# Asking once for the sums of an up pair at a group border

## The chip, the cores and the metric

The kernel runs on one core of a Trainium2 chip. TensorE (PE) multiplies, VectorE (DVE), ScalarE (ACT) and GpSimd (POOL) do the rest, and SyncE (SP) and POOL issue most transfers. The metric is the device time of one execution in microseconds; the time before is the median of three executions.

## The reference

An encoder trunk of four layers over 512 tokens of 1024 features, in float32. Each layer has a token mixer (a convolution module, a neighbourhood attention, a retention, and a convolution module again) and then a channel mixer, the same in all four:

```python
def conv_ffn(h, w_up, dw_w, dw_b, w_down):
    u = dwconv(h @ w_up, dw_w, dw_b)          # 1024 -> 2 x 2816, three taps along the tokens
    val, gate = jnp.split(u, 2, axis=-1)
    return (jax.nn.gelu(gate) * val) @ w_down # 2816 -> 1024
```

with a root-mean-square norm ahead of it and the result added to x. The change is in this channel mixer alone.

## The kernel before, in words

The kernel keeps x on the chip with features on partitions: eight tiles of 128 x 512. Float32 products are made of three matmuls on a high and a low part: ACT casts an operand to its high part (L167, L191), DVE subtracts to get the low part (L168, L192), and PE runs high x high, high x low and low x high (L181 to L183). Some of the up matrices get their low part from a transfer that adds into it on its way (L177, on POOL's queue), and PE uses that part last (L316).

The channel mixer, `ffn`, has 44 blocks of 128 hidden features, taken in 22 pairs j (value and gate). `ups_of(j)` makes pair j; `mids` then runs the three taps and the gate over finished pairs. Two parts of the down product, `down(q, ...)`, are run in between, after pair 8 (9 in the second layer) and after pair 16; these places are called borders here, first and second. Down products, and the four up pairs of each layer that the table `UPS` names, are made with seven products of half blocks instead of eight. For that the weights are needed in sums. `sums` asks for them: a load into `ws` (512 KB, L471, on SP), a transfer that adds another 512 KB into it (L474, on POOL's queue, which waits for that load), and a load of 256 KB into `wq` (L475, on SP). `weights` makes the rest: it loads the plain weights into `wr` (L158), splits them (L167, L168), adds on DVE (L484, and L488 into `wq`) and splits the sums (L191, L192). There are three buffers for `ws` and one for `wq`.

`fetch_sums(j)` calls `sums` one pair ahead and puts what it gets into the dictionary `ahead`, from which `up_macro(j)` takes it. `ups_of(j)` starts with `fetch_sums(j + 1)`.

At a border `down` ends with two calls: `late()`, which runs the taps of pair j, and `filler()`, which is `ups_of(j + 1)`. Then its last output is finished (`finish`: two products, L538 and L515 on DVE, and an addition to x in memory, L539 and L516, on POOL's queue). After that the loop over j goes on and calls `ups_of(j + 1)` once more. Its products were made already, so it makes none; but its first line asks for the sums of pair j + 2 again, and where pair j + 2 is in `UPS` that replaces what the first call had got. That is so for the first pair of `UPS` behind each border: pairs 10 (11 in the second layer) and 18, so twice in each layer.

The order of the work on each engine is set at compile time by a scheduler with a simulated timeline; each engine then works its list in order and waits on semaphores. `issue_after` in `sums` keeps its transfers behind a given load.

Of the kernel before, what the change touches and what calls it, by code (L numbers as in the profile page):

```python
# [77 lines left out]
UPS = ((10, 12, 18, 19), (11, 13, 18, 19), (10, 12, 18, 19), (10, 12, 18, 19))  # L78
# [5 lines left out]
def tile_trunk(  # L84
# [213 lines left out]
    def ffn(l, after):  # L298
        with ExitStack() as st:
# [3 lines left out]
            def up(n):  # L303
                c = n // 2 + FT * (n % 2)
                ps = bank(psa)
                acc = n in ACC
                wh, wl = load_w_acc(f_up[l, c], D) if acc else load_w(f_up[l, c], D)
                for k in range(KD):
                    s = slice(k * P, (k + 1) * P)
                    if acc:  # L310
                        nc.tensor.matmul(ps, wh[:, s], xhi[k], start=k == 0, stop=False)  # L311
                        nc.tensor.matmul(ps, wh[:, s], xlo[k], start=False, stop=False)  # L312
                    else:
                        mm3(ps, wh[:, s], wl[:, s], xhi[k], xlo[k], k == 0, k == KD - 1)
                for k in range(KD if acc else 0):
                    nc.tensor.matmul(ps, wl[:, k * P:(k + 1) * P], xhi[k], start=False, stop=k == KD - 1)  # L316
                if n == 3 and l == 1:
                    stats1(state["spare"])
                if n == S2[l]:
                    stats2()  # L320
                    scale_first()
                if n == SCALED[l] - 1:
                    scale_rest()
                return ps
# [12 lines left out]
            def combos(p):  # L337
                e, o = x[2 * p], x[2 * p + 1]
                c = hp.tile([P, D], F32, tag="ws", name=nm("cx"), bufs=NWS)
                q = [c[:, i * 256:(i + 1) * 256] for i in range(4)]  # L340
                nc.vector.tensor_tensor(q[0], e[:, 256:], e[:, :256], SUB)
                nc.vector.tensor_tensor(q[1], o[:, :256], e[:, :256], SUB)
                nc.vector.scalar_tensor_tensor(q[2], o[:, :256], -1.0, q[0], MUL, SUB)
                nc.vector.scalar_tensor_tensor(q[3], q[2], -1.0, o[:, 256:], MUL, SUB)
                cl[p] = hp.tile([P, D], F32R, tag=f"cl{p}", name=nm("cl"))
                for k, h in ((2 * p, slice(0, T)), (2 * p + 1, slice(T, D))):
                    ch[k] = const.tile([P, T], F32R, tag=f"x{k}", name=nm("ch"))
                    split(c[:, h], ch[k], cl[p][:, h])
# [9 lines left out]
            open_macro, ahead = [], {}  # L358
# [7 lines left out]
            def finish_up():  # L366
                if open_macro:
                    w, v, s12 = open_macro.pop()
                    uprod(v[:, :256], w["sg"], 2, False)
                    uprod(v[:, 256:], w["a12"], 3, True)  # L370
                    nc.vector.tensor_tensor(s12, v, s12, ADD)

            def up_macro(j):
                w = weights(*ahead.pop(j))
                xb, v = bank(psa), bank(psa)
                xc = xb[:, :256]
                s12, u2 = t512(), t512()
                uprod(xc, w["a11"], 1, True)
                nc.scalar.copy(s12[:, 256:], xc)
                uprod(v[:, 256:], w["a22"], 6, True)  # L380
                uprod(xc, w["s2"], 0, False)
                nc.scalar.copy(s12[:, :256], xc)
                uprod(v[:, :256], w["s1"], 4, True)
                uprod(xc, w["s3"], 5, False)
                finish_up()
                nc.scalar.activation(u2.rearrange("p (h t) -> p h t", h=2),
                                     xc.unsqueeze(1).broadcast_to([P, 2, 256]), AF.Copy, scale=-1.0)
                nc.vector.tensor_tensor(u2, u2, v, SUB)
                open_macro.append((w, v, s12))
                return [s12, u2]  # L390
# [75 lines left out]
            def sums(src, gate=None):  # L466
                n = src.shape[-1] // 4
                r13 = hp.tile([P, D], F32, tag="ws", name=nm("ws"), bufs=NWS)
                sg = hp.tile([P, D], F32, tag="wq", name=nm("wq"))
                with tc.issue_after(gate.ins) if gate else ExitStack():  # L470
                    nc.sync.dma_start(  # L471
                        r13[:, :2 * n].rearrange("p (b n) -> p b n", b=2),
                        src[:, 2 * n:3 * n].unsqueeze(1).broadcast_to([P, 2, n]))
                    nc.gpsimd.dma_start(r13[:, :2 * n], src[:, :2 * n], accum_op=ADD)  # L474
                    nc.sync.dma_start(sg[:, n:2 * n], src[:, 3 * n:])  # L475
                return src, r13, sg
# [109 lines left out]
            done, n = 0, 2  # L586
# [6 lines left out]
                    done += 1  # L593

            def fetch_sums(j):
                if j in UPS[l]:
                    ahead[j] = sums(f_us[l, UPS[l].index(j)], state["load"])

            def ups_of(j):
                nonlocal n  # L600
                fetch_sums(j + 1)
                if j in UPS[l]:
                    ups.extend(up_macro(j))
                    n += 2
                while n < 2 * j + 2:
                    ups.append(up(n))
                    finish_up()
                    n += 1
                if j in COMBO:
                    combos(COMBO.index(j))  # L610

            starts = {2 * p1 + (l == 1 and q == 0): q for q, (_, p1) in enumerate(PARTS)}
            for j in range(1, FT):
                ups_of(j)
                w0 = down_w(0, starts[j], state["load"]) if j in starts else None
                if n > S2[l]:
                    mids(j)
                if w0:
                    down(starts[j], w0, lambda: mids(j + 1), lambda: ups_of(j + 1))
# [685 lines left out]
    kind, l = seq[0]  # L1305
# [177 lines left out]
```

## Time and profile before

| | us |
|---|---|
| three executions | 2617.16, 2610.37, 2615.33 |
| median | 2615.33 |
| the profiled execution: its time | 2619.64 |
| its span, first to last instruction | 2617.6 |
| granted TensorE clock, mean over it | 0.988 |

Views of the profile used below: the page (busy time of each engine, DMA queues, the chain of work that ended last), the waits (engine, line, what it waited for; us in total, how often, longest), the chain in order of time (start us, us, what), the timeline of one engine (start us, us, engine, line, operation, tiles; in brackets the idle time before it and what ended it), and the windows (a stretch; its length; busy us of PE, PEld, DVE, ACT and POOL, with the number of instructions; the granted clock; the DMA share; GB/s). "SPq" and "POOL ... DMA" are instructions that issue a transfer; how long it takes to land is in other rows. A line such as L168 is that of a helper and stands for many places.

### The profile page before, as it was taken

To read this page: it belongs to the slowest core of one execution; us is meant where nothing else is said; L and a number is where in the kernel's file an instruction comes from. 1 tells how busy PE (TensorE), PEld (TensorE's weight loads), DVE (VectorE), ACT (ScalarE), POOL (GpSimd) and SP (SyncE) were. 2 spreads that over 40 slices of the span, in tenths; PEclk is the share of its full clock that TensorE was granted. 3 is DMA by queue.
4 is the path that set the end of the run, shared out by engine and by line. 5 is a ranking of instruction groups with operands and counts; after the bars stand their busy time and mean duration, and the time that the engine had idled before them with its cause. 6 is when DMAs were issued, how large, how long until landed. Compare 5 with 4: busy or idle time off the path is not lost.

```text
span 2617.6 us, 38827 instructions
## 1 busy us (share of the span) xinstructions
PE 2543.1 (97%) x15166; PEld 2192.1 (84%) x15166; DVE 1824.9 (70%) x3004; ACT 1264.4 (48%) x1763; POOL 393.9 (15%) x484
## 2 busy tenths in 40 slices
PE   9999999999999999999999999999989999999989
PEld 7888888889998888888888888789888888789787
DVE  7976867577877785657656566685747887686755
ACT  5455545464556554445332423464535445554543
POOL 1214110103421111110000000211011121101010
PEclk9999999999999999999999999999999999999999
DMA  7736776643333567674222222577665672477674
GB/s 240 234 93 189 189 169 173 157 146 97 96 90 109 144 170 172 157 183 123 81 81 72 81 74 75 133 185 183 167 149 140 204 228 83 132 189 173 163 162 138
DMA packets 128521, 381.18 MB, mean 146 GB/s; under 512 B 15521, under 2 KB 18465, under 8 KB 128337
## 3 DMA queue, kind: packets, MB, share of 16 engines
q1 hardware_dynamic: 94144, 283.59, 34.8%
q0 software_dynamic: 32896, 92.39, 19.0%
q10 hardware_dynamic: 1296, 2.72, 0.3%
q8 instruction: 119, 1.95, 0.3%
q14 instruction: 66, 0.53, 0.1%
HBM read 344.07 MB, written 30.79 MB: 143 GB/s over the span
## 4 chain that ended last, share of the span: by engine, by line
PE 80%; DMA 8%; DVE 7%; ACT 3%; issue 2%; POOL 0%; DVEq 0%; SPq 0%; ACTq 0%; POOLq 0%
PE ps L182 19%; PE ps L183 19%; PE ps L181 19%; PE ps L316 3%; PE ps L312 3%; PE ps L311 3%; PE ps L187 3%; PE ps L186 3%; PE ps L188 3%; DMA wr<-in_f_down 2%; DMA wq<-in_f_us 2%; DVE wl L168 2%; DMA wq<-in_f_down 2%; DMA wl<-in_f_up 1%; PE ps L743 1%
## 5 line engine op out<-in xcount | busy, mean ns | idle before, releaser
L167 ACT CAST wh<-wr 128x1024 fp32r<-128x1024 f32 (+1 forms) x310 | 318.0, 1028 | 546.4 <-PE ps L182 264.4
L183 PE MATMUL ps<-xh,wl 128*128 128x512 f32 (+1 forms) x1248 | 486.4, 391 | 11.6 <-DVE wl L168 11.6
L168 DVE TENSOR_TENSOR wl<-wr,wh 128x1024 fp32r<-128x1024 f32 (+1 forms) x307 | 370.6, 1207 | 177.4 <-ACT wh L167 165.9
L182 PE MATMUL ps<-xl,wh 128*128 128x512 f32 (+1 forms) x1248 | 488.2, 391 | 0.3 <-DVE xl L253 0.3
L181 PE MATMUL ps<-xh,wh 128*128 128x512 f32 (+1 forms) x1248 | 486.1, 390 | 0.8 <-ACT wh L167 0.8
L183 PEld LDWEIGHTS ps<-xh,wl 128*128 128x128 f32 x1248 | 235.2, 189 | 67.1 <-DVE wl L168 15.2
L181 PEld LDWEIGHTS ps<-xh,wh 128*128 128x128 f32 x1248 | 235.2, 189 | 54.7 <-ACT wh L167 1.7
L182 PEld LDWEIGHTS ps<-xl,wh 128*128 128x128 f32 x1248 | 235.4, 189 | 52.5 <-DVE xl L253 1.1
L183 PE MATMUL ps<-Hh,wl 128*128 128x256 f32 (+1 forms) x734 | 224.8, 314 | 9.2 <-DVE wl L168 8.8
L182 PE MATMUL ps<-Hl,wh 128*128 128x256 f32 (+1 forms) x734 | 226.8, 313 | 5.6 <-DVE Hl L192 5.6
L181 PE MATMUL ps<-Hh,wh 128*128 128x256 f32 (+1 forms) x734 | 222.5, 315 | 4.9 <-ACT wh L167 2.8
L311 PE MATMUL ps<-xh,wh 128*128 128x512 f32 x416 | 164.7, 396 | 1.3 <-ACT wh L175 1.3
L312 PE MATMUL ps<-xl,wh 128*128 128x512 f32 x416 | 164.4, 395 | 0.0
L187 PE MATMUL ps<-wl,xh 128*128 128x256 f32 (+1 forms) x512 | 159.8, 313 | 1.8 <-DVE wl L168 1.8
L186 PE MATMUL ps<-wh,xh 128*128 128x256 f32 (+1 forms) x512 | 159.8, 315 | 1.1 <-ACT xh L250 1.1
L188 PE MATMUL ps<-wh,xl 128*128 128x256 f32 (+1 forms) x512 | 159.8, 313 | 0.0
L183 PEld LDWEIGHTS ps<-Hh,wl 128*128 128x128 f32 x734 | 141.3, 195 | 18.8 <-DVE wl L168 11.7
L181 PEld LDWEIGHTS ps<-Hh,wh 128*128 128x128 f32 x734 | 140.8, 195 | 17.0 <-ACT wh L167 6.9
L182 PEld LDWEIGHTS ps<-Hl,wh 128*128 128x128 f32 x734 | 141.6, 193 | 14.6 <-DVE Hl L192 7.2
L488 DVE TENSOR_TENSOR wq<-ws,wq 128x512 f32<-128x512 f32 x48 | 33.1, 689 | 138.8 <-DMA wq<-in_f_down 94.3
L181 PE MATMUL ps<-Hh,h 128*128 128x256 f32 x384 | 111.7, 291 | 15.7 <-DVE t L538 15.2
L316 PE MATMUL ps<-xh,wl 128*128 128x512 f32 x416 | 107.9, 401 | 5.3 <-DMA wl<-in_f_up 5.3
(330 smaller groups left out, 6211.1 us busy)
## 6 DMA issues: line engine op xcount, KB each, us to landing
wr<-in_f_up SPq DMA_DIRECT2D x144, 512.0 KB, 4.1
wraw<-in_cdw SPq DMA_DIRECT2D x56, 608.0 KB, 5.2
wl<-in_f_up POOLq DMA_DIRECT2D x52, 512.0 KB, 7.9
ws<-in_f_down SPq DMA_DIRECT2D x32, 512.0 KB, 9.0
wr<-in_f_down SPq DMA_DIRECT2D x32, 512.0 KB, 6.3
ws<-in_f_down POOLq DMA_DIRECT2D x32, 512.0 KB, 7.7
xd<-t POOLq DMA_DIRECT2D x64, 256.0 KB, 7.0
wr<-in_cw_in SPq DMA_DIRECT2D x30, 512.0 KB, 4.0
```

Source lines behind the costliest of these rows:

```text
L167: nc.scalar.copy(hi[:, :n], raw[:, :n])
L168: eng.tensor_tensor(lo[:, :n], raw[:, :n], hi[:, :n].bitcast(F32), SUB)
L181: nc.tensor.matmul(o, wh, ah, start=first, stop=False, skip_group_check=free)
L182: nc.tensor.matmul(o, wh, al, start=False, stop=False, skip_group_check=free)
L183: nc.tensor.matmul(o, wl, ah, start=False, stop=last, skip_group_check=free)
L186: nc.tensor.matmul(o, ah, wh, start=first, stop=False)
L187: nc.tensor.matmul(o, ah, wl, start=False, stop=False)
L188: nc.tensor.matmul(o, al, wh, start=False, stop=last)
L311: nc.tensor.matmul(ps, wh[:, s], xhi[k], start=k == 0, stop=False)
L312: nc.tensor.matmul(ps, wh[:, s], xlo[k], start=False, stop=False)
L316: nc.tensor.matmul(ps, wl[:, k * P:(k + 1) * P], xhi[k], start=False, stop=k == KD - 1)
L488: nc.vector.tensor_tensor(sg[:, :n], r2, sg[:, n:2 * n], ADD)
```

## The change

`fetch_sums` asks only where nothing lies in `ahead` for the pair, and the up pair of seven products is made only where it has not been made.

```diff
             def fetch_sums(j):
-                if j in UPS[l]:
+                if j in UPS[l] and j not in ahead:
                     ahead[j] = sums(f_us[l, UPS[l].index(j)], state["load"])

             def ups_of(j):
                 nonlocal n
                 fetch_sums(j + 1)
-                if j in UPS[l]:
+                if j in UPS[l] and n < 2 * j + 2:
                     ups.extend(up_macro(j))
                     n += 2
```

SP has 605 rows in its list before and 589 now, POOL 330 and 322; PE, DVE and ACT have as many as before.

SP's list at the second border of the first layer, before. `ws` and `wq` from `in_f_us` are the sums of an up pair, from `in_f_down` those of the down product; 4975 and 4976 are the first copy for pair 18 (4975 stands one row ahead of these), 5068 and 5069 the second, 5073 and 5074 pair 19:

```order
L158 DMA wr_4981<-in_f_up 128x1024
L158 DMA wr_5012<-in_f_up 128x1024
L471 DMA ws_5068<-in_f_us 128x2x512
L475 DMA wq_4722<-in_f_down 128x512
L158 DMA wr_5078<-in_f_us 128x1024
L471 DMA ws_5073<-in_f_us 128x2x512
L158 DMA wr_5178<-in_f_us 128x1024
L475 DMA wq_4842<-in_f_down 128x512
L475 DMA wq_4976<-in_f_us 128x512
L475 DMA wq_5069<-in_f_us 128x512
L158 DMA wr_5304<-in_f_up 128x1024
L475 DMA wq_5074<-in_f_us 128x512
```

And with the change (4971 is pair 18's wq, 5063 and 5064 are pair 19's):

```order
L158 DMA wr_4976<-in_f_up 128x1024
L158 DMA wr_5007<-in_f_up 128x1024
L475 DMA wq_4717<-in_f_down 128x512
L158 DMA wr_5068<-in_f_us 128x1024
L471 DMA ws_5063<-in_f_us 128x2x512
L158 DMA wr_5168<-in_f_us 128x1024
L475 DMA wq_4837<-in_f_down 128x512
L475 DMA wq_4971<-in_f_us 128x512
L158 DMA wr_5294<-in_f_up 128x1024
L475 DMA wq_5064<-in_f_us 128x512
```

The second copy's two rows are gone, and the others stand as they stood.

POOL's list at the first border of the second layer, before (`xd` is x in memory, `wl` the low part of an up matrix; 10815 is the second copy's accumulation, 10919 that of pair 13):

```order
L539 DMA xd_113<-t_10434 128x512
L474 DMA ws_10815<-in_f_us 128x1024
L516 DMA xd_114<-t_10371 128x512
L539 DMA xd_115<-t_10554 128x512
L177 DMA wl_10761<-in_f_up 128x1024
L474 DMA ws_10919<-in_f_us 128x1024
L516 DMA xd_116<-t_10491 128x512
```

And with the change (10904 is pair 13's):

```order
L539 DMA xd_113<-t_10424 128x512
L516 DMA xd_114<-t_10361 128x512
L474 DMA ws_10904<-in_f_us 128x1024
L539 DMA xd_115<-t_10544 128x512
L177 DMA wl_10751<-in_f_up 128x1024
L516 DMA xd_116<-t_10481 128x512
```

The accumulation of pair 13 stands ahead of one xd add and of the wl row now, behind both before. At the other borders it has likewise moved ahead of one L539. Behind this border, in the second layer alone, a few of PE's, DVE's and ACT's rows are in another order too.

## The prediction

> **What bounds the kernel now.** I read the page first: the busy shares, the queues and the chain.
>
> ```profile
> PE 2543.1 (97%) x15166; PEld 2192.1 (84%) x15166; DVE 1824.9 (70%) x3004; ACT 1264.4 (48%) x1763; POOL 393.9 (15%) x484
> q1 hardware_dynamic: 94144, 283.59, 34.8%
> q0 software_dynamic: 32896, 92.39, 19.0%
> PE 80%; DMA 8%; DVE 7%; ACT 3%; issue 2%; POOL 0%; DVEq 0%; SPq 0%; ACTq 0%; POOLq 0%
> ```
>
> PE is busy for 97% of 2617.6 us, so all that can be won without taking matmuls away is 74.5 us of idle time, and what a lowered clock adds to the busy time. The wait list of PE says where the idle time is.
>
> ```profile
> PE ps L183 <- DVE wl L168: 20.4, 13, 3.5
> PE ps L181 <- DVE t L538: 15.2, 4, 4.2
> PE ps L316 <- DMA wl<-in_f_up: 5.3, 3, 4.5
> ```
>
> The second row has four waits, one for each layer: each lies at the second border of a layer's channel mixer, where the up pair 18 follows the last product of the first `down` part of that border. I followed the one of layer 0 back, in the chain of waits (start us, us, what).
>
> ```profile
> 481.74 1.15 DVE l L192
> 482.90 10.81 DMA wq<-in_f_down
> 493.80 0.70 DVE wq L488
> 495.74 1.24 DVE l L192
> 496.99 3.43 DMA wq<-in_f_us
> 500.44 4.38 DMA wq<-in_f_us
> ```
>
> A 128x512 load into wq takes 10.81 us; behind it come the sum L488, the split, and then two loads of the same up sums, one after the other, since wq has one buffer: the second is asked for only when the first has landed. The timelines of DVE, PE, SP and POOL at the same place say who stands behind that:
>
> ```profile
> 493.80 0.69 DVE L488 TENSOR_TENSOR wq<-ws,wq 128x512 f32<-128x512 f32 x1 [9.61 <-DMA wq<-in_f_down]
> 498.01 0.68 DVE L538 TENSOR_TENSOR t<-t,ps 128x512 f32<-128x512 f32 x1
> 498.75 0.38 PE L181 MATMUL ps<-Hh,h 128*128 128x256 f32 x1 [4.20 <-DVE t L538]
> 504.94 0.69 DVE L488 TENSOR_TENSOR wq<-ws,wq 128x512 f32<-128x512 f32 x1 [3.67 <-DMA wq<-in_f_us]
> 506.81 1.22 DVE L168 TENSOR_TENSOR wl<-wr,wh 128x1024 fp32r<-128x1024 f32 x1
> 508.08 0.39 PE L183 MATMUL ps<-xh,wl 128*128 128x256 f32 x1 [1.38 <-DVE wl L168]
> 469.97 0.40 SPq L471 DMA_DIRECT2D ws<-in_f_us  x1
> 470.65 0.33 SPq L475 DMA_DIRECT2D wq<-in_f_down  x1
> 479.43 0.38 SPq L471 DMA_DIRECT2D ws<-in_f_us  x1
> 482.90 0.33 SPq L475 DMA_DIRECT2D wq<-in_f_down  x1
> 496.99 3.78 SPq L475 DMA_DIRECT2D wq<-in_f_us  x2
> 478.44 0.88 POOL L474 DMA_DIRECT2D ws<-in_f_us  x1 [8.40 <-DMA ws<-in_f_us]
> 482.03 0.88 POOL L539 DMA_DIRECT2D xd<-t  x1 [0.88 <-DVE t L538]
> 487.73 0.88 POOL L474 DMA_DIRECT2D ws<-in_f_us  x1 [4.82 <-DMA ws<-in_f_us]
> ```
>
> DVE works in order. It stands at L488 for 9.61 us, and L538, which PE needs before it may go on in the same bank, is queued behind: PE waits 4.20 us. Then DVE stands 3.67 us more at the next L488, for the second wq copy, and L168 behind it holds PE for 1.38 us. The load of 469.97 and the accumulation of 478.44 are the second copy of pair 18 (the first was asked for before; 479.43 and 487.73 are pair 19). The price by stage, with PE's busy time and granted clock:
>
> ```profile
> 494.00:518.00 24.00, 17.62 (x122) 16.37 (x121) 16.91 (x22) 11.43 (x16) 2.56 (x3) 0.93 0.52 112
> 1135.00:1157.00 22.00, 16.08 (x103) 15.39 (x102) 14.67 (x19) 9.55 (x14) 2.59 (x3) 0.84 0.57 114
> 1949.00:1973.00 24.00, 17.18 (x119) 15.99 (x119) 16.56 (x22) 12.37 (x18) 2.59 (x3) 0.93 0.52 111
> 2525.00:2547.00 22.00, 15.41 (x102) 15.00 (x101) 13.83 (x19) 10.28 (x15) 2.59 (x3) 0.84 0.51 105
> ```
>
> The columns are the stretch, its length, then busy us of PE, PEld, DVE, ACT and POOL, the clock, the DMA share and GB/s. PE is idle for 6.38, 5.92, 6.82 and 6.59 us: 25.7 us in the four second borders. The clock was 0.93, 0.84, 0.93 and 0.84, so matmuls ran longer as well: one minus the clock, times the busy time, gives 1.2 + 2.6 + 1.2 + 2.5 = 7.5 us; times the whole stretch, 10.4 us. I take 9. So these stretches have 34.7 us to give, 33.2 to 36.1.
>
> **The change part by part.** *What goes.* Eight second copies, two in each layer: a load of 512 KB into ws and one of 256 KB into wq on SP, and an accumulation of 512 KB on POOL's queue. That is 16 rows of SP and 8 of POOL, and 10.5 MB of 381 MB. The second edit, the guard on `n`, takes nothing away: no pair of the list is reached twice. No matmul, cast or vector instruction goes. From the queue rows, q1 spends 0.348 x 2617.6 / 283.59 = 3.2 us of all engines per MB and q0 0.190 x 2617.6 / 92.39 = 5.4 us. So a copy costs 1.7 us (ws), 0.8 us (wq) and 2.8 us (accumulation) of the DMA engines, 5.3 in all.
>
> *Second border, first wait.* The load of 469.97 stands in SP's queue ahead of the wq load of 470.65, so that one lands 1.7 us earlier without it, and everything strung on it (L488, the split, the load of 482.90) moves by 1.7 us, to 481.2. Of the 10.81 us that the next wq load takes, the accumulation of 478.44 is worth up to 2.8 us. It lands at 493.7 - 1.7 - 2.8 = 489.2 and L538 starts at 498.01 - 4.5 = 493.5 and ends at 494.2. PE comes there at 498.75 - 4.20 = 494.55. The wait is gone, with 0.4 us to spare in layer 0 and more in the others, whose waits are 3.7 on average. Bounds: 1.7 us alone leaves 2.5 of 4.2 standing; and the order of POOL can help, since the surviving L474 now stands ahead of the L539 of 482.03, and nothing but one xd add runs on q0 until pair 19's load has landed, which gives the wq load the engines for itself.
>
> *Second border, second wait.* The first copy's wq load is asked for at 496.99 - 4.5 = 492.5 and takes 3.43 us, to 495.9; there is no second one (4.38 us). L488, at 504.94 now, waits for nothing then: DVE work ahead of it ends some 4.5 us earlier than now, at 496.7, and L168 follows 1.87 us behind L488, so it ends at 499.8. PE gets there at 506.70 (508.08 - 1.38) less the 4.2 won and at least 1.2 of clock (0.31 of 4 us, in the next fence): 501.3. That wait goes too. What SP issues behind the second copy goes out earlier by the copy's 4.38 us as well, so nothing new is late behind it.
>
> *The clock.* These rows are of 4 us each:
>
> ```profile
> 498.00:502.00 4.00, 3.25 (x18) 3.25 (x19) 3.27 (x6) 2.05 (x3) 0.85 (x1) 0.69 0.87 155
> 506.00:510.00 4.00, 2.62 (x22) 2.42 (x22) 4.00 (x6) 3.17 (x5) 0.03 (x1) 1.00 0.02 4
> 1151.00:1155.00 4.00, 3.62 (x17) 3.62 (x18) 4.00 (x6) 2.09 (x4) 0.86 (x1) 0.57 0.28 23
> ```
>
> After the idle 4.20 us the clock was 0.69; with the 1.38 us wait inside it stayed 1.00. In layer 1 a stretch that holds no more than 0.4 us of idle time had 0.57. So short gaps can cost clock as well, and I don't count the clock as won for a gap that is halved. The Trainium skill (TensorE: Matmul & The Clock Gate, "Part 1: The HAM clock gate") says that the array falls to half rate after about one idle window of 3.4 us, and that the window runs free. By that rule a rest of 1 to 2 us would cost no clock at all, and the 9 us would be won even where a wait is only halved; the row of layer 1 does not bear that out.
>
> Of the 34.7 us I take 29 as won: small rests will stay, and PE arriving 8 us earlier will meet some wait that is hidden now. All that it needs next (the up loads of SP, DVE's and ACT's work) is strung on the same loads and moves along.
>
> *First borders.* There the same second copies exist. In layers 0, 2 and 3 little waits behind them: 0.8 us of the L316 row (5.3 less 4.5) and some waits for wl, of which I take 1 us in all. In layer 1 it is one wait of 4.5:
>
> ```profile
> 1001.00:1013.00 12.00, 7.45 (x32) 6.24 (x32) 9.13 (x12) 3.96 (x6) 1.75 (x2) 0.72 1.00 211
> 979.97 8.79 DMA ws<-in_f_us
> 990.24 0.38 SPq L471 DMA_DIRECT2D ws<-in_f_us  x1
> 992.39 13.56 DMA wl<-in_f_up
> 998.12 0.88 POOL L474 DMA_DIRECT2D ws<-in_f_us  x1 [4.32 <-DMA ws<-in_f_us]
> wl<-in_f_up POOLq DMA_DIRECT2D x52, 512.0 KB, 7.9
> ```
>
> The second copy's load (979.97) held POOL at its accumulation, and the accumulation into wl (L177) behind it went out at 992.39 and took 13.56 us. But here the order changes: the L474 of pair 13, at 998.12 now, will stand ahead of L177. Its load (990.24 now) may go out 1.7 us earlier (988.5), and takes 7.9 us as now or 5.1 without the copy's accumulation: L474 at 993.6 to 996.4, L177 some 2 us behind at 995.5 to 998.3, landing 7.9 us (the median) to 13.56 us later: 1003.4 to 1011.9, against 1005.95 now. So between 2.5 won and 6 lost, and the clock with it; the queue is emptier, which puts me at 1005.4: 0.5 won.
>
> Sum: 29 + 1 + 0.5 = 30.5 us. The profiled execution took 2619.64 us (span 2617.6); less 30.5 that is 2589.1. It lies 4.3 us above the median of the three runs (2615.33), so I put the median after at 2585.
>
> The Trainium skill (DMA: Bandwidth & Descriptors, "Anatomy of one DMA") fits a transfer as 2 us that don't scale and bytes over 436 GB/s. By that, taking a 524 KB transfer out of a full queue frees an estimated 1.2 us, not 1.7 and 2.8, and the L538 waits shrink by 2.4 us each instead of vanishing; the two queue rows speak for the longer figures, though they may hold time in which packets waited for each other.
>
> **The rivals.**
>
> *Half of it.* The wq load is late mostly for what stays: pair 19's ws, an f_us load and two xd adds. Then 2.4 us come off each of the four waits (15.2 to 5.6), half of the clock's 9 comes back, and of the later waits some 5: 9.6 + 4.5 + 5 = 19, the time 2596. For it: those are issued in the same 11 us, and 482.90 is behind pair 19's ws (479.43) in SP's queue. Against it: POOL's surviving accumulation moves out of the way. The rule of the DMA page falls in here.
>
> *No change.* wq's 10.81 us hang on what stays, and the second wq copy's 4.4 us of DVE standing turn into standing at the next load of wq, as each needs the split of the one before. Then only the first borders' 1 us and a few waits come: under 7 us, 2609 to 2615. Against it is the chain above, which runs through the second copy itself.
>
> *Slower.* POOL works in order, and at every border one more xd add (L539), in layer 1 the wl accumulation too, now stands behind an L474 that waits for its load (8.40 us at 478.44). The add of 482.03 would go out when pair 19's load has landed, about 486: 4 us late, and with it its t tile comes free, of which the stage has seven. If all seven are in use, ACT's copy out of the bank waits, and PE behind it. 4 us at eight borders are 32 us: that eats the gain (2617), and makes 2647 where the gain doesn't come. It decides only if t tiles run short; none of the three rows of PE's waits is for a t tile to come free.
>
> *That it does nothing* is excluded: the rows of SP and POOL are 16 and 8 fewer.
>
> **How the numbers follow.** My forecast 0.64 (2574 to 2593 as its own range: all of it, 36.1 and in the first borders 4.6 + 3.4 + 1, gives 2570, 22 gives 2593), half of it 0.21 (2593 to 2605), no change 0.09, slower 0.06. Within 0.3%, about 8 us, is what a measurement of this kernel can't tell from no change. So faster by more than that, below 2607.5, is 0.85; same 0.09; slower 0.06. The range for 8 in 10 goes from 2572, short of the ceiling, to 2604, the end of the half case.
>
> **What would show it.** Right: in the changed profile PE's row for L538 falls from 15.2 us to under 3; the wq<-in_f_down load at the second border takes 6 to 9 us instead of 10.8, and L488 has one wait for wq<-in_f_us there of under 2 us; the clock in those stretches is 0.97 or more; SP has one wq<-in_f_us where now are two 3.4 us apart; ws<-in_f_us counts 16 instead of 24. Half: L538 still at 5 to 7 us. Wrong: the L538 row stands at 12 or more, or new rows appear in PE's waits that name a t tile, xd, or, in layer 1, L316 with more than 8 us.

## The result, and the profile after

| | before | after |
|---|---|---|
| median of the executions, us | 2616.24 (2610.37 to 2619.45) | 2579.89 (2579.26 to 2581.99) |
| the profiled execution: its time, us | 2619.64 | 2579.95 |
| its span, us | 2617.6 | 2577.9 |
| granted TensorE clock, mean over it | 0.988 | 0.993 |

The changed kernel is faster: the ratio is 0.9865, with a 95% interval of 0.9846 to 0.9884, and the medians lie 36.4 us apart. The prediction had 2585 us: the direction and the place were right, and the gain of 30.5 us that it worked out was some 6 us short.

The page of the changed kernel, in the order in which that of before was read (busy times, queues, shares of the chain), and its issue rows for the sums:

```profile
PE 2528.4 (98%) x15166; PEld 2182.9 (85%) x15166; DVE 1826.8 (71%) x3004; ACT 1265.2 (49%) x1763; POOL 387.2 (15%) x476
q1 hardware_dynamic: 90816, 277.30, 34.2%
q0 software_dynamic: 31744, 88.19, 18.4%
PE 86%; DVE 6%; DMA 4%; ACT 2%; issue 1%; DVEq 0%; POOL 0%; SPq 0%; ACTq 0%; POOLq 0%
ws<-in_f_us SPq DMA_DIRECT2D x16, 512.0 KB, 6.0
```

The matmuls are as many as before, 15166, and yet PE is busy for 14.7 us less (2543.1 to 2528.4): they ran at a higher clock. Its idle time fell by 25.0 us (74.5 to 49.5). The two make the 39.7 us between the two spans. That it is the clock fits the table: one minus the mean clock, times the span, is 31.4 us before and 18.0 after, 13.4 less. DMA's share of the chain halved, 8% to 4%, and `ws<-in_f_us` counts 16, so the copies are gone.

PE's waits after (engine, line, what it waited for; us in total, how often, longest):

```profile
PE ps L183 <- DVE wl L168: 7.6, 3, 2.9
PE ps L181 <- ACT Hh L191: 6.3, 3, 2.9
PE ps L316 <- DMA wl<-in_f_up: 3.3, 1, 3.3
```

The row for L538 (15.2 us, four waits) no longer exists, the row for wl has 3 waits instead of 13, and L316 lost 2.0 us. A row that was short before has grown: the wait for Hh, cast on ACT.

The same four second borders as in the prediction's windows, in the changed kernel's own time (stretches of the same length; the fourth begins some 6 us earlier in the work than its match did):

```profile
486.50:510.50 24.00, 24.00 (x164) 22.09 (x163) 19.33 (x27) 14.96 (x21) 2.68 (x4) 1.00 0.63 139
1119.00:1141.00 22.00, 22.00 (x165) 20.96 (x165) 16.66 (x22) 10.76 (x15) 3.75 (x5) 1.00 0.70 152
1918.00:1942.00 24.00, 24.00 (x176) 22.72 (x176) 17.19 (x22) 12.10 (x17) 3.46 (x4) 1.00 0.70 149
2483.00:2505.00 22.00, 22.00 (x160) 20.73 (x160) 15.90 (x20) 10.71 (x15) 4.40 (x5) 1.00 0.80 168
```

PE is busy in every microsecond of them, at a clock of 1.00, and in the fourth layer without a gap from 2450 to 2520 us. Before it was idle for 25.7 us in these stretches, at 0.84 to 0.93. The timelines of DVE, PE, SP and POOL in the first layer answer to those that the prediction showed:

```profile
485.81 0.69 DVE L488 TENSOR_TENSOR wq<-ws,wq 128x512 f32<-128x512 f32 x1 [3.05 <-DMA wq<-in_f_down]
490.03 0.68 DVE L538 TENSOR_TENSOR t<-t,ps 128x512 f32<-128x512 f32 x1
493.83 0.69 DVE L488 TENSOR_TENSOR wq<-ws,wq 128x512 f32<-128x512 f32 x1 [0.54 <-DMA wq<-in_f_us]
492.96 0.28 PE L181 MATMUL ps<-Hh,h 128*128 128x256 f32 x1
475.75 0.38 SPq L471 DMA_DIRECT2D ws<-in_f_us  x1
479.21 0.33 SPq L475 DMA_DIRECT2D wq<-in_f_down  x1
489.00 0.33 SPq L475 DMA_DIRECT2D wq<-in_f_us  x1
482.58 0.88 POOL L474 DMA_DIRECT2D ws<-in_f_us  x1 [5.10 <-DMA ws<-in_f_us]
483.13 1.20 POOL L539 DMA_DIRECT2D xd<-t  x1
```

The load into wq goes out at 479.21 and takes 6.50 us, where it took 10.81 (5.2 to 6.5 us in the four layers, where it was 9.2 to 10.8); L488 starts at 485.81. DVE stands there for 3.05 us instead of 9.61. L538 ends at 490.71, and PE comes to the product that needs it at 492.96, without a wait. The next L488 waits 0.54 us for the one load of `in_f_us` instead of 3.67 for the second of two.

### The profile page after: what moved, and what is told of

Same layout as the page of the kernel before. It is cut to its first block, busy times and chain, and to the rows that moved or that the text cites. A ratio compares the mean times of both kernels' runs of the same rounds, so it can differ in the third digit from the quotient of the medians.

```text
span 2577.9 us, 38787 instructions
## 1 busy us (share of the span) xinstructions
PE 2528.4 (98%) x15166; PEld 2182.9 (85%) x15166; DVE 1826.8 (71%) x3004; ACT 1265.2 (49%) x1763; POOL 387.2 (15%) x476
## 4 chain that ended last, share of the span: by engine, by line
PE 86%; DVE 6%; DMA 4%; ACT 2%; issue 1%; DVEq 0%; POOL 0%; SPq 0%; ACTq 0%; POOLq 0%
PE ps L182 21%; PE ps L183 21%; PE ps L181 21%; PE ps L316 3%; PE ps L312 3%; PE ps L311 3%; PE ps L187 3%; PE ps L188 3%; PE ps L186 3%; DMA wr<-in_f_down 2%; DVE wl L168 1%; PE ps L743 1%; PE ps L742 1%; PE ps L741 1%; PE ps L454 1%
## 5 line engine op out<-in xcount | busy, mean ns | idle before, releaser
L183 PEld LDWEIGHTS ps<-Hh,wl 128*128 128x128 f32 x734 | 142.0, 196 | 17.5 <-DVE wl L168 10.5
L182 PEld LDWEIGHTS ps<-Hl,wh 128*128 128x128 f32 x734 | 142.7, 195 | 15.3 <-DVE Hl L192 7.8
L177 POOL DMA_DIRECT2D wl<-in_f_up x52 | 46.7, 897 | 451.1 <-ACT wl L176 401.9
L316 PE MATMUL ps<-xh,wl 128*128 128x512 f32 x416 | 107.8, 400 | 3.3 <-DMA wl<-in_f_up 3.3
```

The source lines that it names most:

```text
L177: nc.gpsimd.dma_start(lo[:, :n], src.bitcast(F32R), accum_op=ADD)
L182: nc.tensor.matmul(o, wh, al, start=False, stop=False, skip_group_check=free)
L183: nc.tensor.matmul(o, wl, ah, start=False, stop=last, skip_group_check=free)
```

## The experiments

All kernels but `xd_first`, `behind_wl`, `after_again` and `gate_down` are the kernel before with one edit, and those four start from the changed kernel. The theory: the gain comes from the second borders, in two parts that lie one behind the other. The wq load of the down product becomes early enough for L538 (through the ws load and the accumulation that are gone), and then the second wq copy no longer holds DVE. Rivals: the first borders have a share; the bytes count and not their place; the new order on POOL does it; one of the three transfers does it alone. In kernels with an added line the numbers are one higher (L539 is L538, L489 is L488).

### One border alone

The second copies are left out at the second borders alone, or at the first borders alone. The first edit is `second_only`, the other `first_only`.

```diff
-                if j in UPS[l]:
+                if j in UPS[l] and not (j == 18 and j in ahead):
...
-                if j in UPS[l]:
+                if j in UPS[l] and not (j < 18 and j in ahead):
```

> The second copies are left out at the four second borders (pair 18) and kept at the four first ones. My theory (the gain is the four L538 waits, the later wl waits and the clock behind them, all at second borders): 32 to 36 us below the kernel before, ratio about 0.987, as the whole change; L538 no longer in PE's wait list. Rival (each of the eight copies costs the same, whatever stands behind it): 18 us, ratio 0.993.

> The second copies are left out at the four first borders and kept at the second ones. My theory: 1 to 4 us below the kernel before, ratio 0.9985 to 1.000; L538 stays at about 15 us in PE's waits, L316 at 3 to 4. Rival (equal shares): 18 us, ratio 0.993.

Second borders alone: 2580.56 against 2615.69, ratio 0.9864 (0.9843 to 0.9886), the whole of the gain. First borders alone: 2615.33, ratio 1.0003 (0.9991 to 1.0015), nothing at all. PE's waits with the first borders alone:

```profile
PE ps L181 <- DVE t L538: 12.7, 4, 4.0
PE ps L181 <- ACT Hh L191: 8.6, 4, 3.6
PE ps L316 <- DMA wl<-in_f_up: 3.5, 1, 3.5
```

and with the second borders alone:

```profile
PE ps L316 <- DMA wl<-in_f_up: 5.3, 3, 4.3
PE ps L181 <- ACT Hh L191: 2.5, 2, 1.3
```

So the change at the first borders does shorten L316 (5.3 to 3.5), and it brings the wait for Hh (1.7 before, 2.5 without it, 8.6 with it). In the time nothing is left of what the first borders win.

### One transfer of the copy alone

Three kernels keep the second call and leave out a part of the copy. `copy_ws` leaves out only its wq load, `copy_wq` keeps only its wq load, and `copy_no_acc` leaves out only the accumulation (its sums lack one term there).

```diff
-            def sums(src, gate=None):
+            def sums(src, gate=None, old=None):
...
-                sg = hp.tile([P, D], F32, tag="wq", name=nm("wq"))
+                sg = old[2] if old else hp.tile([P, D], F32, tag="wq", name=nm("wq"))
...
-                    nc.sync.dma_start(sg[:, n:2 * n], src[:, 3 * n:])
+                    if not old:
+                        nc.sync.dma_start(sg[:, n:2 * n], src[:, 3 * n:])
...
                 if j in UPS[l]:
-                    ahead[j] = sums(f_us[l, UPS[l].index(j)], state["load"])
+                    ahead[j] = sums(f_us[l, UPS[l].index(j)], state["load"], ahead.get(j))
```

(That is `copy_ws`; the other two put `if not old` around the ws load and the accumulation, keeping the old ws tile, or around the accumulation alone.)

> Of the second copy only the 256 KB load into wq is left out; its 512 KB load into ws and its accumulation stay, and POOL's list is that of the kernel before. My theory (two causes, the ws traffic for the L538 wait, the second wq load for the wl wait behind it): L538 stays at 13 to 15 us in PE's waits with its clock, the wl waits behind it go; 10 to 16 us below the kernel before, ratio about 0.995. Rival A (the second wq load, which can only be asked for when the first has landed, is the whole cause): 33 us or more, ratio 0.987. Rival B (the wq load costs nothing): within 3 us.

> Of the second copy only the load into wq stays; the ws load and the accumulation are left out, and POOL's list is that of the changed kernel. My theory: L538 is gone from PE's waits; the second wq load lands 3.4 us after the first, which PE now reaches late enough that at most 1 to 2 us of waiting for wl come back at each second border: 28 to 36 us below the kernel before, ratio 0.986 to 0.989. Rival A (the second wq load is the whole cause): within 8 us of the kernel before.

> The second copy keeps its load into ws and its load into wq, but not its accumulation, so the sums that the up pairs behind the borders use lack one term; the amount of other work is the same. SP's list is that of the kernel before, POOL's that of the changed one but for two rows. My theory (the accumulation is worth up to 2.8 of the 10.81 us of the wq load, the ws load ahead of it 1.7): the L538 waits shrink to 0 to 1.5 us each, the second wq copy stays; 20 to 30 us below the kernel before, ratio 0.989 to 0.992. Rival (the ws load in SP's own queue is what makes wq late, the accumulation runs beside it): L538 stays at 10 us or more, gain under 10 us, ratio above 0.996.

`copy_ws`: 2600.2 against 2615.69, ratio 0.9948 (0.9931 to 0.9965). Its waits, and from its chain the wq load:

```profile
PE ps L181 <- DVE t L539: 11.6, 4, 3.5
PE ps L183 <- DVE wl L168: 8.1, 4, 2.9
485.06 9.40 DMA wq<-in_f_down
```

The load still takes 9.40 us and the L538 waits stand at 11.6 us (13 to 15 had been expected), while the wl waits are down to 8.1 from 20.4: what came is in the main the second part, and 3.6 us of the L538 row. The time is inside what was expected.

`copy_wq`: 2594.73, ratio 0.9921 (0.9903 to 0.994), against 28 to 36 us expected. 21.0 us came. The L538 waits are gone as the theory has it. Its waits, and DVE and PE in the first layer:

```profile
PE ps L183 <- DVE wl L168: 17.3, 11, 2.9
499.42 0.70 DVE L489 TENSOR_TENSOR wq<-ws,wq 128x512 f32<-128x512 f32 x1 [4.06 <-DMA wq<-in_f_us]
502.56 0.39 PE L183 MATMUL ps<-xh,wl 128*128 128x256 f32 x1 [1.18 <-DVE wl L168]
```

DVE stands 4.06 us at the second copy's L488 here too, and 11 wl waits remain (17.3 us; 3 with 7.6 in the changed kernel). The smallest of the three transfers, 256 KB, keeps some 15 us of the 36.

`copy_no_acc`: 2601.47 against 2616.79, ratio 0.9939 (0.9919 to 0.996); 20 to 30 us had been expected, 15.3 came. From its chain, PE's timeline and its waits:

```profile
483.79 5.79 DMA wq<-in_f_down
505.22 0.39 PE L183 MATMUL ps<-xh,wl 128*128 128x256 f32 x1 [3.68 <-DVE wl L168]
PE ps L183 <- DVE wl L168: 22.1, 9, 3.7
```

Without the accumulation the wq load takes 5.79 us, although the ws load still stands ahead of it in SP's queue, and no wait for L538 is left. (POOL's list has the new order here, so this is not the accumulation's doing alone.) But PE then meets the second wq copy, and waits 3.68 us for wl where it had waited 1.38. The two waits are in series: taking the first away alone lengthened the second. The gains of `copy_ws` and `copy_wq`, which between them leave out each transfer once, add up to the whole (15.5 + 21.0).

### The same bytes at the other place

`drop_first` leaves out the first copy instead of the second: as many transfers as in the changed kernel, asked for where the second stood.

```diff
-            def ups_of(j):
+            def ups_of(j, fetch=True):
                 nonlocal n
-                fetch_sums(j + 1)
+                if fetch:
+                    fetch_sums(j + 1)
...
-                    down(starts[j], w0, lambda: mids(j + 1), lambda: ups_of(j + 1))
+                    down(starts[j], w0, lambda: mids(j + 1), lambda: ups_of(j + 1, False))
```

> The first copy is left out instead of the second: one copy as in the changed kernel, the same bytes, but asked for where the second one stood in the kernel before, ahead of the down product's wq load in SP's list. My theory (it is the place of the transfers that costs, ahead of the wq loads on which L488 stands): L538 stays at 10 to 15 us in PE's waits, only the wl waits behind it go; 10 to 18 us below the kernel before, ratio 0.993 to 0.996. Rival (the number of bytes through the DMA engines is what counts): as the changed kernel, 33 us or more, ratio 0.987.

2598.55 against 2616.79, ratio 0.9928 (0.9911 to 0.9945): 18.2 us, half of the gain. Its waits, chain and PE's timeline:

```profile
PE ps L181 <- DVE t L538: 15.5, 4, 4.5
482.33 11.07 DMA wq<-in_f_down
498.44 0.38 PE L181 MATMUL ps<-Hh,h 128*128 128x256 f32 x1 [4.50 <-DVE t L538]
```

The bytes of the changed kernel and the wait of the kernel before: the wq load takes 11.07 us, as the surviving ws load and accumulation go out right beside it. The other half of the gain, which does not come here, is one of place and not of bytes.

### The order on POOL

`xd_first` is the changed kernel, but at the second borders POOL has to issue pair 19's accumulation behind the L539 that stood ahead of it before the change.

```diff
-            def sums(src, gate=None):
+            def sums(src, gate=None, xfirst=None):
...
-                    nc.gpsimd.dma_start(r13[:, :2 * n], src[:, :2 * n], accum_op=ADD)
+                    with tc.issue_after(xfirst.ins) if xfirst else ExitStack():
+                        nc.gpsimd.dma_start(r13[:, :2 * n], src[:, :2 * n], accum_op=ADD)
...
-                    nc.gpsimd.dma_start(xd[2 * i], u2, accum_op=ADD)
+                    state[f"xd{i}"] = nc.gpsimd.dma_start(xd[2 * i], u2, accum_op=ADD)
...
-                    ahead[j] = sums(f_us[l, UPS[l].index(j)], state["load"])
+                    ahead[j] = sums(f_us[l, UPS[l].index(j)], state["load"], state["xd2"] if j == 19 else None)
```

> The changed kernel, but at the four second borders POOL is made to issue pair 19's accumulation (L474) behind the xd add (L539) that stood ahead of it in the kernel before; nothing else differs in any list. It tells whether the L538 wait went because the second copy's accumulation is gone (my theory: then the wq load still takes 6 to 8 us at that place, L538 is not in PE's waits or under 3 us in all, and the time is within 4 us of the changed kernel, ratio 0.985 to 0.988), or because the surviving accumulation moved behind the wq load's way and the xd add with it (rival: wq takes 9 us or more again, L538 comes back with 8 us or more, ratio 0.991 or above).

2580.18 against 2616.95, ratio 0.9854 (0.9838 to 0.9871): the gain is whole, and no wait for L538 comes back. Its chain has

```profile
479.66 7.40 DMA wq<-in_f_down
```

so the order is worth some 0.9 us of that load (7.40 against 6.50) and nothing in the time, and the second copy's transfers together are worth the other 3.4 us (10.81 to 7.40).

### The first border of the second layer

There POOL now issues pair 13's accumulation ahead of the one into wl, and one L316 wait of 3.3 us stands. `behind_wl` asks for pair 13's sums behind pair 12's up loads. `after_again` is the changed kernel unaltered, beside it on the same chip.

```diff
-                fetch_sums(j + 1)
+                late = l == 1 and j == 12
+                if not late:
+                    fetch_sums(j + 1)
...
+                if late:
+                    fetch_sums(j + 1)
```

> The changed kernel, with one thing more: in the second layer the sums of pair 13 are asked for behind the up loads of pair 12, so that on POOL's list the accumulation into wl (L177) stands ahead of that pair's L474 again, as in the kernel before, without the second copy in front. My theory (POOL's order holds L177 back): L177 goes out 4 to 6 us earlier at that border and the 3.3 us L316 wait and its lowered clock go: 3 to 6 us below the changed kernel, ratio to the kernel before about 0.985. Rival (the landing of wl is bound by the bytes, not by when it is asked for): within 1.5 us of the changed kernel.

> The changed kernel as it is, on the same chip as the next one: 0.9865 of the kernel before, L316 3.3 us in PE's waits.

2580.88 and 2577.9, ratios 0.9863 (0.9848 to 0.9878) and 0.9855 (0.9837 to 0.9873): nothing won. The wait is gone at its place and stands one pair later. PE and POOL:

```profile
1018.93 2.50 PE L316 MATMUL ps<-xh,wl 128*128 128x512 f32 x5 [3.91 <-DMA wl<-in_f_up]
1004.63 0.90 POOL L474 DMA_DIRECT2D ws<-in_f_us  x1 [8.29 <-DMA ws<-in_f_us]
1008.64 0.89 POOL L177 DMA_DIRECT2D wl<-in_f_up  x1 [0.96 <-ACT t L382]
```

The first L177 went out only 2.1 us earlier (981.11 against 983.16; 4 to 6 had been expected). POOL then stands 8.29 us at the accumulation of pair 13, and the next L177 goes out at 1008.64, 1.9 us later than in the changed kernel. So the order does move the wait, but the theory that the order costs the time fell: the wait was handed on. Why the later load of wl lands too late was not tried.

### A version that beats both

The rows that grew led to the loads of `in_f_down`: in the changed kernel ACT waits 5.50 us for a wr at the start of the second layer's second part. `gate_down` is the changed kernel with one row of SP moved at each part: the first down product's plain load into wr goes ahead of the ws loads of the second and third product.

```diff
-                    w = down_w(i, q) if i else first
+                    if i == 0:
+                        gate = state["load"]
+                    w = down_w(i, q, gate) if i else first
```

> The changed kernel, with the lesson tried at another place: at the start of each down part the first product's plain weights (wr) are asked for ahead of the sums' loads (ws) of the second and third product, behind which they stand in SP's list now; nothing else moves but that row. My theory (the place in the queue is what costs): the first wr<-in_f_down load of a part, 9 to 15 us in the chain of waits, takes 5 to 9; PE's waits at the starts of the second parts (wl L168, Hh, Hl, some 15 us in all with the clock) shrink; 4 to 14 us below the changed kernel, ratio to the kernel before 0.980 to 0.984. Rival (what is put back, ws of the second product, turns into the next wait, or the H tiles are what PE waits for there): within 3 us of the changed kernel, ratio 0.985 to 0.987.

2567.61 against 2616.95, ratio 0.9811 (0.9797 to 0.9826): 10.3 and 12.3 us below the two medians of the changed kernel (2577.9 and 2579.89), inside the 4 to 14 us expected. ACT's timeline, the issue rows, and two stretches at the start of a second part, first in the changed kernel:

```profile
1060.75 1.05 ACT L167 CAST wh<-wr 128x1024 fp32r<-128x1024 f32 x1 [5.50 <-DMA wr<-in_f_down]
ws<-in_f_down SPq DMA_DIRECT2D x32, 512.0 KB, 8.5
wr<-in_f_down SPq DMA_DIRECT2D x32, 512.0 KB, 6.2
1055.00:1085.00 30.00, 23.41 (x109) 20.00 (x108) 21.69 (x28) 11.37 (x14) 2.19 (x3) 0.83 0.60 149
2427.00:2457.00 30.00, 26.32 (x138) 23.25 (x137) 21.62 (x28) 13.10 (x15) 0.87 (x1) 0.83 0.52 139
```

and then in `gate_down`:

```profile
1052.60 1.05 ACT L167 CAST wh<-wr 128x1024 fp32r<-128x1024 f32 x1 [0.72 <-DMA wr<-in_f_down]
ws<-in_f_down SPq DMA_DIRECT2D x32, 512.0 KB, 6.8
wr<-in_f_down SPq DMA_DIRECT2D x32, 512.0 KB, 5.1
1055.00:1085.00 30.00, 25.02 (x153) 22.50 (x152) 21.68 (x27) 11.47 (x14) 2.62 (x3) 0.89 0.67 167
2427.00:2457.00 30.00, 26.76 (x208) 25.92 (x207) 19.72 (x24) 12.85 (x18) 3.52 (x4) 0.94 0.59 145
```

ACT's 5.50 us are 0.72, and the clock there is 0.89 and 0.94 instead of 0.83. Over the execution PE is idle for 4.5 us less and, with as many matmuls, busy for 9.3 us less (2519.1). Most of that is the clock: its mean over the span, 0.993 before and 0.996 here, makes 7.8 us. Not all of the theory held: PE's wait for Hh did not shrink (6.3 us in the changed kernel, 6.8 here).

## Why the prediction was right, and where its size was off

- **Second border, first wait: right.** The wq load takes 6.50 us (6 to 9 had been named), L538 ends ahead of PE, its row is gone. Both terms were put too small. The load came to its issue 2.3 us earlier behind the one before it (9.99 us apart where it was 12.25), and 1.7 had been forecast. The load itself lost 4.3 us, and 2.8 had been forecast: 3.4 of them for the second copy's transfers, 0.9 for the order on POOL. So there were 2.2 us to spare in the first layer where "0.4" was forecast, and it did not hang on luck.
- **Second border, second wait: right.** It is the second wq copy; `copy_wq` shows what it keeps when all else is gone. What I had wrong, in two of the expectations, was how little this wait would cost once the first is gone: `copy_wq` won 21.0 us and not 28 to 36, `copy_no_acc` 15.3 and not 20 to 30. The second wq load is worth some 15 us either way, left out alone (15.5) or kept alone.
- **"Of the 34.7 us I take 29 as won": this is the term that was off.** No rest stayed in those stretches; all 25.7 us of idle time went, so the discount of 5.7 us had nothing to stand for; it is the larger part of the miss. PE did meet a wait that was hidden, as the discount supposed, but elsewhere and for less. I compared four stretches, each with one channel mixer and, in the first three layers, work of the next token mixer behind it. Outside the four windows their idle time (length less PE's busy time) went from 39.6 to 40.0 us. The largest rise lies in the second layer ahead of its second border, before:

```profile
840.60:1135.00 294.40, 284.09 (x1588) 246.40 (x1588) 198.86 (x277) 147.96 (x193) 43.51 (x46) 0.97 0.67 166
```

 and after:

```profile
829.20:1119.00 289.80, 278.76 (x1550) 241.70 (x1549) 199.42 (x277) 147.56 (x193) 40.59 (x44) 0.97 0.63 158
```

 that is 10.3 and 11.0 us idle. The four stretches became shorter by 10.5, 7.4, 12.0 and 8.9 us, the second layer's least. PE's list has another order in the second layer alone, so that order is not what the gain comes from.
- **The clock was the other part of the miss.** I took 9 us, for the four stretches alone. In the four stretches with the mixers PE's busy time fell by 13.5 us, so also outside the windows. A part may be that the profiled execution of before lies 3.4 us above its median; that is not shown.
- **First borders: 1 and 0.5 us forecast, nothing came.** The L316 wait in the second layer went from 4.5 to 3.3 us, inside the bounds, and the wait for Hh in that layer from 1.2 to 4.9. `second_only` keeps it at 1.2 there and `first_only` has 5.9, so it is shown that the first border's change brings it. By which transfer is not shown: asking for wr earlier (`gate_down`) still leaves 3.8 us.
- **The sum.** 25.7 of idle time less 0.5, and 13.5 of clock, are the 38.7 us of the four stretches in the two profiled executions; the medians say 36.4, the prediction 30.5. The 8.2 us between 38.7 and 30.5 are the discount (5.7) and the clock (4.5), less the first borders' 1.5 that did not come and the 0.5.
- **The rivals.** Half of it: fell, though it is what half of the change gives (`copy_ws`, `copy_no_acc`, `drop_first`: 15 to 18 us, 19 forecast). No change: fell. Slower through POOL: at the second border of the first layer the L539 does stand behind an L474 that waits 5.10 us, and no wait of PE or ACT names xd; `xd_first`, with that order undone at the second borders, takes the same time. The price of this rival counted eight borders, and the section on the change speaks of all the others too, but the surviving accumulation moved ahead of an L539 at five alone: in POOL's timelines the first borders of the first, third and fourth layer lose the second copy's row and keep the order of the rest.

On the clock the prediction had a row against a rule: 0.57 in a stretch of the second layer with no more than 0.4 us of idle time in it. PE had waited 1.89 us just ahead of that, in the kernel before:

```profile
1151.38 0.50 PE L183 MATMUL ps<-xh,wl 128*128 128x256 f32 x1 [1.89 <-DVE wl L168]
```

The runs have two more. PE and windows of `copy_ws`, at the second borders of the second and third layer:

```profile
1140.33 0.39 PE L181 MATMUL ps<-Hh,h 128*128 128x256 f32 x1 [2.23 <-DVE t L539]
1139.00:1143.00 4.00, 2.67 (x22) 2.67 (x23) 4.00 (x7) 2.49 (x4) 0.86 (x1) 1.00 0.78 137
1143.00:1147.00 4.00, 4.00 (x36) 4.00 (x35) 4.00 (x7) 2.50 (x5) 0.00 (x0) 1.00 0.56 173
1944.13 0.39 PE L181 MATMUL ps<-Hh,h 128*128 128x256 f32 x1 [2.46 <-DVE t L539]
1944.00:1948.00 4.00, 3.87 (x20) 3.87 (x21) 4.00 (x8) 1.57 (x2) 0.86 (x1) 0.58 0.73 142
```

A wait of 2.23 us cost no clock, while 2.46 us were followed by 4 us at 0.58, in which PE had hardly an idle moment, and 1.89 us by 0.57. The price falls behind the wait, and whether it falls is not told by the length. The Trainium skill (TensorE: Matmul & The Clock Gate, "Part 1: The HAM clock gate") has half rate after one or more idle windows of about 3.4 us; the level of 0.58 fits half rate over most of the stretch, but 2.46 us of idle time were enough here, so the length does not agree.

PE's wl and L538 waits are 3 now and were 17, so it pays that price less often; that this makes the clock's 13.5 us is argued, and no run measured it by itself.

On the transfers the queue rows were nearer than the rule. By the Trainium skill (DMA: Bandwidth & Descriptors, "Anatomy of one DMA"), whose fit is for transfers that GpSimd issues, the accumulation's 524 KB make an estimated 1.2 us. The wq load beside it lost 3.4 us in `xd_first`, and in `copy_no_acc` 5.0, which less the 0.9 us of the order is an estimated 4.1, so that here the measured figures decide against it.

## What to carry to other kernels

Look in the chain of waits for the same tile loaded twice in a row: a transfer whose data nobody reads still holds its buffer, its queue and whoever stands behind it in order. Price it by the wait of the engine that works in order, not by its bytes: half of this gain would have stayed behind if the bytes had gone and the place had not. And when two waits stand in series, an edit that removes one can lengthen the other (1.38 to 3.68 us here). Take the whole stretch, idle time and clock, as the prize, and count it as won only where every wait in it has lost its cause; where that was so, here, no rest stayed and a discount was too careful.

## What the runs showed of the hardware

A 256 KB load on SP's queue took 10.81 us beside an accumulating transfer of 512 KB on POOL's queue. It took 7.40 without the second copy's transfers and with POOL's old order (`xd_first`), and 5.79 without the accumulation alone and with the new order (`copy_no_acc`), of which the order is some 0.9. That makes the accumulation an estimated 3.4 to 4.1 us, more than the 2.8 us that its share of the queue's time gave. A wait of some 2 us can cost nearly as much again in a lowered clock right behind it, and can cost nothing (0.58 and 1.00 for 4 us after 2.46 and 2.23 us). And moving one row in SP's list, with all transfers kept, was worth 10 to 12 us (`gate_down`), about a third of what this change gave by leaving 10.5 MB out.
